# A decoder trunk in three-term fp32r products: the first tile pairs of each feed forward, the weight combinations and the result sums rearranged

## The chip, the cores and the metric

The kernel runs on 1 core of one Trainium2 chip. The metric is device time in microseconds, the median of 3 runs; smaller is better. Engines in the profile: PE (TensorE's matmuls), PEld (its weight loads), DVE (VectorE), ACT (ScalarE), POOL (GpSimd), SP (SyncE, which issues most of the DMAs here).

## What is computed

A trunk of two decoder layers over 512 tokens of 1024 features in float32. Each layer is feed forward, token mixing, feed forward, each with a residual and a layer norm. The first layer mixes by latent attention, the second by sparse attention on keys and values made from the output of the first. The change touches the four feed forwards:

```python
def swiglu(x, w_gu, w_down):
    g, u = jnp.split(x @ w_gu, 2, axis=-1)
    return (jax.nn.silu(g) * u) @ w_down
...
    for layer in range(DEPTH):
        x = layer_norm(DN_ALPHA * x + 0.5 * swiglu(x, ffn_w_gu[layer, 0], ffn_w_down[layer, 0]), ...)
        ... token mixing, w_out, layer_norm ...
        x = layer_norm(DN_ALPHA * x + 0.5 * swiglu(x, ffn_w_gu[layer, 1], ffn_w_down[layer, 1]), ...)
        if layer == N_A_LAYERS - 1:
            shared = nsa_shared_kv(x, ...)
```

with D_FF = 2816, so gate and up are 22 tiles of 128 hidden features each.

## The kernel before, in words

**Products.** Every float32 operand is kept as two fp32r parts, hi (a rounded copy, by ScalarE's cast, L198) and lo (the rest, by VectorE's subtraction, L199); `split` (L194) makes both. A product is three matmuls: hi by hi, hi by lo, lo by hi. The input of a feed forward lies feature-major in `F.xhi` and `F.xlo` (1024 features in 8 blocks of 128, by 512 tokens), and, unsplit, as four raw blocks `F.raw[k, c]` (feature half k, token half c).

**A feed forward** (`ffn`, L456) works through 22 tile pairs (a gate tile and an up tile of 128 hidden features each) in five groups. After each group its down projection adds to the residual (`token_major`, `by_units`, L420 to 453). `GROUPS` (L33) says for each pair of each feed forward which of two ways makes it:

- "s", a plain pair (`single`, L476): two weight units of 128x1024, each `feature_major` (L354): 24 matmuls of 256 columns for each token half, so 96 in all.
- "d", a combined pair (`seven`, L484): a fast multiplication of the 2x2 block matrices (feature halves by token halves), with seven block products of 12 matmuls (`quarter`, L370), 84 in all. Its left operands are g0 to g3: the gate block, the up block and four combinations of their halves (`combined`, L132; four operations of 512 columns on VectorE, in place in the raw weight tiles). Its right operands are `F.xhi`/`F.xlo` quarters and the token forms `F.t[1]` to `F.t[4]`, combinations of the raw blocks (`token_forms`, L385; four subtractions of 1024 columns and four splits). Seven sums of 256 columns on VectorE and one copy on ScalarE put the results together (L494 to 512); then `evac` (L470): Silu on ScalarE, a product on VectorE and a split.

**The front of a feed forward.** The norm that makes the input runs one tile of 128 tokens after the other (`norm_tile`, L318), with transposes on TensorE (L338), so the second token half comes later than the first. In the first, second and fourth feed forward (`halves`, L518 to 534) three plain pairs open: six weight units, first all six on tokens 0 to 255, then all six on tokens 256 to 511. The token forms come behind that, between the next products. The third feed forward reads an `x` that has been there since before the stage ahead of it (`shared_kv`, the keys and values of the second layer); it opens with two plain pairs, and its token forms are started in `shared_kv` (L935).

**Weights.** `unit` (L176) hands out the weight units in the order of `_unit_order` (L53) and prepares up to `look` more ahead (`ahead`, L184; `prep`, L153): a load of 512 KB on SP's queue into one of 4 raw tiles (`wraw`), a cast and a lo subtraction into one of 7 slots. The token forms' subtractions use raw tiles too.

**The start.** The program loads the transposed input in eight pieces (L1262) with one weight unit ahead of it and three between its halves (L1264). The hook `load_x` (L1272) of the first feed forward loads the token-major `x` (four loads pinned to program order) and then the norm's gain and bias, behind the six units of the front.

**What sets the order.** Engines run lists that the compiler orders by readiness with the program's order as priority; tiles of a pool are handed out in program order. PSUM has eight banks, used in turn (`fbank`).

Of the kernel before, what the change touches and what calls it, by code (L numbers as in the profile page):

```python
# [52 lines left out]
def _unit_order():  # L53
# [3 lines left out]
    def ffn(l, f, s):  # L57
        for m0, items in _groups(l, f):
            m = m0
            for it in items:  # L60
# [4 lines left out]
                m += 1  # L65
            for i in range(m0, m):
                order.append(("dn", (l, f, i), 1024, s))
# [36 lines left out]
def tile_trunk(ctx: ExitStack, tc, a: dict, out):  # L104
# [27 lines left out]
    def combined(name, idx):  # L132
# [129 lines left out]
    def open_f(scope):  # L262
# [11 lines left out]
        for i in (1, 2, 3, 0, 4):  # L274
# [181 lines left out]
    def ffn(l, f, i, halves, spill=None, final=False, mid=None, hook=None):  # L456
# [3 lines left out]
        groups = _groups(l, f)  # L460
        for gi, (m0, items) in enumerate(groups):
# [8 lines left out]
            def evac(j, pg, pu, sg=None):  # L470
                sg = sg or hp.tile([P, T], F32, tag="sg", name="sg", bufs=3)
                nc.scalar.activation(sg, pg, AF.Silu)
                nc.vector.scalar_tensor_tensor(sg, sg, 0.5, pu, op0=ALU.mult, op1=ALU.mult)
                split(hhi[:, j, :], hlo[:, j, :], sg)

            def single(j):  # L476
                pp = []
                for g in range(2):
                    w = unit("gu", (l, f, m0 + j, g), 4)
                    pp.append(fbank())  # L480
                    feature_major(w, pp[g], 0, T)
                evac(j, *pp)

            def seven(j):  # L484
# [50 lines left out]
            for it in items:  # L535
                if gi == 0:
                    next(forms, None)
# [934 lines left out]
```

## Time and profile before

| | |
|---|---|
| median of 3 runs | 1878.33 us |
| the runs | 1875.61, 1878.33, 1878.87 us |
| the profiled execution | 1874.17 us, its span 1872.2 us |
| PE, PEld busy | 99%, 88% of the span |
| DVE, ACT, POOL busy | 78%, 46%, 9% |
| mean granted TensorE clock | 0.997 of full speed |

The profile is of one execution. Times in it are us from the span's start. "Busy" counts the time an engine has an instruction in work; matmuls are pipelined, so that the start of one to the start of the next is what one costs, and the printed duration is longer. In a timeline row, `x8` means eight such instructions in a row, and the bracket at the end is the engine's idle time before it and what released it.

### The profile page before, as it was taken

Reading aid. Unit: us, or ns where it says so; the run is one execution under the profiler, and the core shown is the slowest. Engines: PE = TensorE matmul, PEld = TensorE weight load, DVE = VectorE, ACT = ScalarE, POOL = GpSimd, SP = SyncE. Lnnn points to the kernel's source line nnn. Section 1 sums busy time; section 2 is a strip of 40 time slices with the busy share of each in tenths; the row PEclk is TensorE's granted clock in tenths of the full one; section 3 lists DMA queues with packets and bytes.
Section 4 is the critical chain, followed back from the end, with each engine's and each line's share of the span. In section 5 each row is a group of like instructions: output and inputs, shape, how many; then the busy total and the mean of one; then the engine's idle time right before and its main releaser. Section 6 shows DMA issues by size and latency. Waiting matters only on the chain.

```text
span 1872.2 us, 31918 instructions
## 1 busy us (share of the span) xinstructions
PE 1844.3 (99%) x12776; PEld 1650.9 (88%) x12776; DVE 1466.2 (78%) x2362; ACT 869.8 (46%) x1435; POOL 164.2 (9%) x185
## 2 busy tenths in 40 slices
PE   9999999999999999999999999999999999999998
PEld 8899899986679899899999998998956689999997
DVE  8788789757658789788797987987577478888887
ACT  5344345456545345334653433444466345434432
POOL 0000000125500000000100000001255200000000
PEclk9999999999999999999999999999999999999999
DMA  6333335521134234234433323334321224323322
GB/s 245 112 109 126 101 113 158 174 89 35 57 113 136 79 102 136 80 103 145 129 117 113 124 81 112 113 123 154 107 46 28 88 83 146 102 91 113 113 81 78
DMA packets 59700, 203.85 MB, mean 109 GB/s; under 512 B 6944, under 2 KB 7216, under 8 KB 59552
## 3 DMA queue, kind: packets, MB, share of 16 engines
q1 hardware_dynamic: 57136, 194.70, 31.7%
q0 software_dynamic: 2416, 7.11, 1.2%
q8 instruction: 101, 1.65, 0.4%
q14 instruction: 47, 0.39, 0.1%
HBM read 188.16 MB, written 7.34 MB: 104 GB/s over the span
## 4 chain that ended last, share of the span: by engine, by line
PE 92%; DVE 3%; ACT 2%; POOL 1%; issue 1%; DMA 0%; SPq 0%; POOLq 0%; DVEq 0%; ACTq 0%
PE bank L375 13%; PE bank L379 13%; PE bank L376 13%; PE bank L411 5%; PE bank L414 5%; PE bank L412 5%; PE bank L410 5%; PE bank L413 4%; PE bank L415 4%; PE bank L367 3%; PE bank L364 3%; PE bank L362 3%; PE o L645 3%; PE tb L617 3%; PE s L1153 1%; PE bank L352 1%
## 5 line engine op out<-in xcount | busy, mean ns | idle before, releaser
L198 ACT CAST whi<-wraw 128x1024 fp32r<-128x1024 f32 (+3 forms) x479 | 463.2, 976 | 539.2 <-PE bank L415 244.3
L199 DVE TENSOR_TENSOR wlo<-wraw,whi 128x1024 fp32r<-128x1024 f32 (+3 forms) x479 | 536.3, 1126 | 126.6 <-ACT whi L198 125.1
L375 PE MATMUL bank<-t,whi 128*128 128x256 f32 x1232 | 298.4, 278 | 0.0
L376 PE MATMUL bank<-t,whi 128*128 128x256 f32 x1232 | 297.9, 278 | 0.0
L376 PEld LDWEIGHTS bank<-t,whi 128*128 128x128 f32 x1232 | 231.8, 188 | 0.0
L375 PEld LDWEIGHTS bank<-t,whi 128*128 128x128 f32 x1232 | 231.8, 188 | 0.0
L376 PE MATMUL bank<-xlo,whi 128*128 128x256 f32 x924 | 221.9, 277 | 0.0
L375 PE MATMUL bank<-xhi,whi 128*128 128x256 f32 x924 | 221.8, 277 | 0.0
L379 PE MATMUL bank<-t,wlo 128*128 128x256 f32 x1232 | 191.8, 278 | 0.0
L375 PEld LDWEIGHTS bank<-xhi,whi 128*128 128x128 f32 x924 | 173.6, 188 | 0.6
L376 PEld LDWEIGHTS bank<-xlo,whi 128*128 128x128 f32 x924 | 173.6, 188 | 0.6
L379 PEld LDWEIGHTS bank<-t,wlo 128*128 128x128 f32 x1232 | 164.2, 189 | 0.0
L314 DVE SCALAR_TENSOR_TENSOR x<-x,bank 128x512 f32<-128x512 f32 x176 | 112.6, 683 | 57.1 <-PE bank L414 54.3
L379 PE MATMUL bank<-xhi,wlo 128*128 128x256 f32 x924 | 142.9, 277 | 0.0
L411 PE MATMUL bank<-whi,hhi 128*128 128x512 f32 x336 | 131.0, 390 | 0.0
L413 PE MATMUL bank<-wlo,hhi 128*128 128x512 f32 x336 | 130.9, 390 | 0.0
L410 PE MATMUL bank<-whi,hhi 128*128 128x512 f32 x336 | 130.8, 390 | 0.0
L414 PE MATMUL bank<-whi,hlo 128*128 128x512 f32 x336 | 130.8, 389 | 0.0
L412 PE MATMUL bank<-wlo,hhi 128*128 128x512 f32 x336 | 130.8, 389 | 0.0
L362 PE MATMUL bank<-xhi,whi 128*128 128x256 f32 x544 | 130.1, 280 | 0.7 <-ACT xhi L198 0.7
L364 PE MATMUL bank<-xlo,whi 128*128 128x256 f32 x544 | 130.2, 280 | 0.5 <-DVE xlo L199 0.5
L415 PE MATMUL bank<-whi,hlo 128*128 128x512 f32 x336 | 130.7, 389 | 0.0
(330 smaller groups left out, 3548.8 us busy)
## 6 DMA issues: line engine op xcount, KB each, us to landing
wraw<-in_gu SPq DMA_DIRECT2D x175, 512.0 KB, 3.3
wraw<-in_dn SPq DMA_DIRECT2D x88, 512.0 KB, 3.7
wraw<-in_wo SPq DMA_DIRECT2D x16, 512.0 KB, 3.3
wraw<-in_wm SPq DMA_DIRECT2D x8, 512.0 KB, 4.1
x_dram<-x SPq DMA_DIRECT2D x8, 512.0 KB, 3.0
x<-x_dram SPq DMA_DIRECT2D x8, 512.0 KB, 4.4
wraw<-in_w SPq DMA_DIRECT2D x8, 512.0 KB, 4.1
wraw<-in_wq SPq DMA_DIRECT2D x6, 512.0 KB, 3.3
```

The lines of the kernel that those rows point to most:

```text
L198: nc.scalar.copy(hi, src)
L199: eng.tensor_tensor(lo, src, hi.bitcast(F32), op=ALU.subtract)
L364: nc.tensor.matmul(ps[:, c0:c1], lhsT=hi[:, k * P:(k + 1) * P], rhs=F.xlo[:, k, c0:c1], start=False, stop=False)
L375: nc.tensor.matmul(ps, lhsT=hi[:, ks], rhs=xh[:, k], start=k == 0, stop=False)
L376: nc.tensor.matmul(ps, lhsT=hi[:, ks], rhs=xl[:, k], start=False, stop=False)
L379: nc.tensor.matmul(ps, lhsT=lo[:, ks], rhs=xh[:, k], start=False, stop=k == 3)
L410: nc.tensor.matmul(p0, lhsT=ahi, rhs=hi[:, 0:512], start=first, stop=False)
L411: nc.tensor.matmul(p1, lhsT=ahi, rhs=hi[:, 512:1024], start=first, stop=False)
L412: nc.tensor.matmul(p0, lhsT=ahi, rhs=lo[:, 0:512], start=False, stop=False)
L413: nc.tensor.matmul(p1, lhsT=ahi, rhs=lo[:, 512:1024], start=False, stop=False)
L414: nc.tensor.matmul(p0, lhsT=alo, rhs=hi[:, 0:512], start=False, stop=last)
L415: nc.tensor.matmul(p1, lhsT=alo, rhs=hi[:, 512:1024], start=False, stop=last)
```

## The change

- Every feed forward has the same groups, and its first group is one plain pair and four combined ones. Seven plain pairs in all become combined.
- `front` opens each feed forward, the third too: two weight units; the hook; both units on tokens 0 to 255; then `early(1)`, the two quarter products of the next pair that need only g0 and tokens 0 to 255; then the four token forms; then both units on tokens 256 to 511, the plain pair's `evac`, and the rest of the next pair (`seven(1, ...)`). The token forms are no longer spread between products, and those of the third feed forward are no longer started in `shared_kv`.
- The weight combinations add where they subtracted; the signs move to the token forms (two of them by the operation with a scalar, `neg`) and to the factor of `evac`.
- The seven sums of 256 columns become three over 512 columns and one over 256, with the products placed in banks to match (`p15`, `p26`, `p4`, `p37`), and ScalarE's copy stands behind the products with t1, t4 and t2. The two tiles of sums become one of twice the size.
- At the start two units, not three, are prepared between the halves of the transposed input.
- The forms' places in `open_f` are listed in another order.

```diff
@@ -30,14 +30,13 @@
 DMA_RING = 4096
 NRAW, NRING, NEXTRA = 4, 3, 4
 EXTRA = (0, 2, 4, 6)
-GROUPS = (("sssdd", "dddd", "ddddd", "dddd", "dddd"), ("sssdd", "dddd", "ddddd", "dddd", "dddd"),
-          ("ssddd", "dddd", "ddddd", "dddd", "dddd"), ("sssdd", "dddd", "ddddd", "dddd", "dddd"))
-
-
-def _groups(l, f):
+GROUPS = ("sdddd", "dddd", "ddddd", "dddd", "dddd")
+
+
+def _groups():
 
     m, out = 0, []
-    for items in GROUPS[2 * l + f]:
+    for items in GROUPS:
         out.append((m, items))
         m += len(items)
     assert m == NFF
...
@@ -141,13 +138,13 @@
         if name == "g1":
             W.u = load(a["gu"][l, f, m, 1])
             W.s = wraw.tile([P, 1024], F32, name="wraw")
-            op(W.s[:, up], W.g[:, lo], W.u[:, lo], op=ALU.subtract)
+            op(W.s[:, up], W.g[:, lo], W.u[:, lo], op=ALU.add)
             op(W.u[:, lo], W.u[:, lo], W.u[:, up], op=ALU.add)
             return W.u
         if name == "g2":
-            op(W.s[:, lo], W.u[:, lo], W.g[:, lo], op=ALU.subtract)
+            op(W.s[:, lo], W.u[:, lo], W.g[:, lo], op=ALU.add)
             return W.s
-        op(W.g[:, up], W.g[:, up], W.s[:, lo], op=ALU.subtract)
+        op(W.g[:, up], W.g[:, up], W.s[:, lo], op=ALU.add)
         return W.g[:, up]
 
     def prep():
...
@@ -271,7 +268,7 @@
         W.count = 0
         F.fst = ExitStack()
         F.fm = F.fst.enter_context(tc.tile_pool(name=f"fm{scope}", bufs=1, reuse_waits="tile"))
-        for i in (1, 2, 3, 0, 4):
+        for i in (2, 3, 4, 0, 1):
             for e in "hl":
                 if i:
                     F.fm.tile([P, 4, 256], F32, tag=f"t{i}{e}", name="place")
...
@@ -384,9 +381,12 @@
 
     def token_forms():
 
-        def less(x, y):
+        def less(x, y, neg=False):
             u = wraw.tile([P, 1024], F32, name="wraw").rearrange("p (k q) -> p k q", k=4)
-            nc.vector.tensor_tensor(u, x, y, op=ALU.subtract)
+            if neg:
+                nc.vector.scalar_tensor_tensor(u, x, -1.0, y, op0=ALU.mult, op1=ALU.subtract)
+            else:
+                nc.vector.tensor_tensor(u, x, y, op=ALU.subtract)
             return u
 
         def form(i, u):
...
@@ -394,16 +394,12 @@
             split(*F.t[i], u)
 
         b, F.t = F.raw, {}
-        u = less(b[0, 1], b[0, 0])
+        u = less(b[0, 0], b[0, 1])
         form(1, u)
-        yield
-        u = less(b[1, 1], u)
+        u = less(u, b[1, 1], True)
         form(2, u)
-        yield
-        u = less(u, b[1, 0])
-        form(4, u)
-        u = less(b[1, 1], b[0, 1])
-        form(3, u)
+        form(4, less(u, b[1, 0], True))
+        form(3, less(b[1, 1], b[0, 1]))
 
     def prod(ps, w, a, first, last):
         (hi, lo), (ahi, alo), (p0, p1) = w, a, ps
...
@@ -467,82 +463,77 @@
                 F.bk += 1
                 return bank(F.bk - 1)
 
...
+            def hidden():
+                return hp.tile([P, 2, T], F32, tag="sg", name="sg", bufs=2)
+            def evac(j, sg, pg, pu, sign):
                 nc.scalar.activation(sg, pg, AF.Silu)
...
+                nc.vector.scalar_tensor_tensor(sg, sg, 0.5 * sign, pu, op0=ALU.mult, op1=ALU.mult)
                 split(hhi[:, j, :], hlo[:, j, :], sg)
 
...
+            c0, c1 = slice(0, 256), slice(256, 512)
+            def early(j):
                 w = unit("g0", (l, f, m0 + j), 4)
...
+                p15, p26 = fbank(), fbank()
+                quarter(p15[:, c0], w, 0, *quarters(0, 0))
+                quarter(p26[:, c0], w, 512, *quarters(1, 0))
+                return p15, p26
+            def seven(j, p15, p26):
+                both = hidden()
+                gs, us = both[:, 0], both[:, 1]
+                h = both.rearrange("p a (b q) -> p (a b) q", b=2)
+                def sums(o, x, y):
+                    nc.vector.tensor_tensor(o, x, y, op=ALU.add)
+                def twice(x):
+                    return x[:, None, :].to_broadcast([P, 2, 256])
+                def banked(p):
+                    return p.rearrange("p (b q) -> p b q", b=2)
                 w = unit("g1", (l, f, m0 + j), 4)
...
+                p4, p37 = fbank(), fbank()
+                quarter(p15[:, c1], w, 0, *F.t[1])
+                quarter(p4[:, c0], w, 512, *F.t[4])
                 w = unit("g2", (l, f, m0 + j), 4)
...
+                quarter(p26[:, c1], w, 0, *F.t[2])
+                nc.scalar.copy(h[:, 2], p15[:, c0])
+                sums(h[:, 0:4:3], twice(h[:, 2]), banked(p26))
+                quarter(p37[:, c1], w, 512, *F.t[3])
                 w = unit("g3", (l, f, m0 + j), 4)
...
+                quarter(p37[:, c0], w, 0, *quarters(1, 1))
+                sums(h[:, 1:3], twice(h[:, 3]), banked(p37))
+                sums(h[:, 1:4:2], h[:, 1:3], twice(p15[:, c1]))
+                sums(h[:, 2], h[:, 2], p4[:, c0])
+                evac(j, gs, gs, us, -1)
+            def front():
+                ws = [unit("gu", (l, f, m0, g), 0) for g in range(2)]
+                ps = [fbank() for _ in range(2)]
                 if hook is not None:
                     hook()
                     load_gb(l, i, nc.sync)
                 for c in range(2):
                     for w, p in zip(ws, ps):
                         feature_major(w, p, c * 256, c * 256 + 256)
...
+                    if c == 0:
+                        pp = early(1)
+                        token_forms()
+                evac(0, hidden()[:, 0], *ps, 1)
+                seven(1, *pp)
+            if gi == 0:
+                front()
+            for j in range(2 if gi == 0 else 0, n):
+                seven(j, *early(j))
 
             last = gi == len(groups) - 1
             if gi == 2 and mid is not None:
...
@@ -932,7 +923,6 @@
         nc.gpsimd.dma_start(b1, a["cmp_b1"].to_broadcast([64, 2, 256]))
         ws = [unit("wkf", (i,), 4) for i in range(4)]
         ps = [bank(i) for i in range(4)]
-        F.forms = token_forms()
         for c in range(2):
             for i in range(4):
                 feature_major(ws[i], ps[i], c * 256, c * 256 + 256)
...
@@ -1263,7 +1253,7 @@
                 k = slice(e * 4 + i.start, e * 4 + i.stop)
                 split(F.xhi[:, k, q], F.xlo[:, k, q], xr[:, i])
         if c == 0:
-            for i in range(3):
+            for i in range(2):
                 prep()
     sst.close()
     nc.vector.tensor_copy(cbf[:, 0:256], cst[:, 0:256])
...
@@ -1292,11 +1282,11 @@
     open_f(1)
     out_proj(0)
     mst.close()
-    ffn(0, 1, 2, True)
+    ffn(0, 1, 2)
     zst, zp = right_pool("zp")
     shared_kv(zp)
     zst.close()
-    ffn(1, 0, 0, False, spill=x_dram[1])
+    ffn(1, 0, 0, spill=x_dram[1])
     F.fst.close()
     F.mix = {}
     mst, F.mp = right_pool("mix1")
...
@@ -1315,7 +1305,7 @@
     open_f(2)
     out_proj(1)
     mst.close()
-    ffn(1, 1, 2, True, final=True)
+    ffn(1, 1, 2, final=True)
     F.fst.close()
     close_f()
     PS.left_st.close()
```

The lines that the long hunk takes out (`single`, `seven` and the old front) are in the listing above.

## Rows read from the trace of the kernel before

**Rows 1.** The page's first part: busy us (share of span), instructions by engine

```profile
PE 1844.3 (99%) x12776; PEld 1650.9 (88%) x12776; DVE 1466.2 (78%) x2362; ACT 869.8 (46%) x1435; POOL 164.2 (9%) x185
```

**Rows 2.** The page's chain that ended last, by engine

```profile
PE 92%; DVE 3%; ACT 2%; POOL 1%; issue 1%; DMA 0%; SPq 0%; POOLq 0%; DVEq 0%; ACTq 0%
```

**Rows 3.** Timeline of PE, first and second front: start us, us, engine, line, operation

```profile
18.68 1.07 PE L367 MATMUL bank<-xhi,wlo 128*128 128x256 f32 x8
...
21.40 1.07 PE L367 MATMUL bank<-xhi,wlo 128*128 128x256 f32 x8
22.30 0.28 PE L362 MATMUL bank<-xhi,whi 128*128 128x256 f32 x1
...
594.71 0.28 PE L375 MATMUL bank<-xhi,whi 128*128 128x256 f32 x1
...
604.31 0.28 PE L375 MATMUL bank<-xhi,whi 128*128 128x256 f32 x1
```

**Rows 4.** Timeline of PE, second and fourth front, around the last token tiles

```profile
560.71 0.36 PE L362 MATMUL bank<-xhi,whi 128*128 128x256 f32 x1
...
570.34 1.06 PE L338 MATMUL bank<-cst,x 128*128 128x128 f32 x8
571.15 0.36 PE L364 MATMUL bank<-xlo,whi 128*128 128x256 f32 x1
...
1526.07 0.28 PE L362 MATMUL bank<-xhi,whi 128*128 128x256 f32 x1
...
1528.59 0.36 PE L364 MATMUL bank<-xlo,whi 128*128 128x256 f32 x1
...
1537.04 1.09 PE L338 MATMUL bank<-cst,x 128*128 128x128 f32 x8
```

**Rows 5.** Timeline of DVE, second front: the last token tile and the forms

```profile
571.62 1.29 DVE L199 TENSOR_TENSOR xlo<-bank,xhi 128x512 fp32r<-128x512 f32 x2 [1.37 <-ACT xhi L198]
572.97 1.23 DVE L389 TENSOR_TENSOR wraw<-b 128x1024 f32<-128x1024 f32 x1
...
575.44 1.22 DVE L199 TENSOR_TENSOR t<-wraw,t 128x1024 fp32r<-128x1024 f32 x1
...
577.71 1.22 DVE L199 TENSOR_TENSOR t<-wraw,t 128x1024 fp32r<-128x1024 f32 x1
...
579.98 2.48 DVE L199 TENSOR_TENSOR t<-wraw,t 128x1024 fp32r<-128x1024 f32 x2
```

**Rows 6.** Timeline of SP's queue and of ACT at the start

```profile
0.73 0.87 SPq L129 DMA_DIRECT2D wraw<-in_gu  x2
...
15.06 0.33 SPq L297 DMA_DIRECT2D b<-in_ln_b  x1
...
9.86 1.05 ACT L198 CAST whi<-wraw 128x1024 fp32r<-128x1024 f32 x1 [0.58 <-DMA wraw<-in_gu]
```

**Rows 7.** DMA issues: tensor, queue, count, KB each, us from issue to landing

```profile
b<-in_ln_b SPq DMA_DIRECT2D x1, 512.0 KB, 11.2
```

**Rows 8.** Timeline of DVE, behind the second front: sums, combination, hidden product

```profile
616.08 0.41 DVE L506 TENSOR_TENSOR us<-us,bank 128x256 f32<-128x256 f32 x1
616.41 0.42 DVE L512 TENSOR_TENSOR gs<-gs,bank 128x256 f32<-128x256 f32 x1
...
618.54 0.69 DVE L150 TENSOR_TENSOR wraw<-wraw 128x512 f32<-128x512 f32 x1
619.14 0.69 DVE L473 SCALAR_TENSOR_TENSOR gs<-gs,us 128x512 f32<-128x512 f32 x1
```

**Rows 9.** Timeline of PE, where the third feed forward opens

```profile
949.46 0.31 PE L994 MATMUL bank<-cst,hb 64*128 64x64 f32 x2 [2.42 <-DVE hb L991]
...
954.16 1.73 PE L367 MATMUL bank<-xhi,wlo 128*128 128x256 f32 x8
```

**Rows 10.** Two stretches: us, busy us (xcount) by engine, granted clock, DMA share, GB/s

```profile
561.00:614.00 53.00, 53.00 (x465) 52.99 (x464) 46.94 (x61) 29.92 (x41) 1.71 (x3) 1.00 0.39 130
952.00:966.00 14.00, 14.00 (x111) 13.72 (x109) 12.60 (x22) 6.21 (x14) 0.00 (x0) 0.88 0.12 37
```

More of the change, by code (lines that the diff above doesn't have):

```diff
@@ L57, in ffn @@
     def ffn(l, f, s):
-        for m0, items in _groups(l, f):
-            m = m0
-            for it in items:
+        for m0, items in _groups():
+            for m, it in enumerate(items, m0):
                 if it == "d":
@@ L64, in ffn @@
                     order.extend(("gu", (l, f, m, g), 1024, s) for g in range(2))
-                m += 1
-            for i in range(m0, m):
-                order.append(("dn", (l, f, i), 1024, s))
+            for m in range(m0, m0 + len(items)):
+                order.append(("dn", (l, f, m), 1024, s))
     ffn(0, 0, 0)
@@ L453, in by_units, with ffn @@
                         on_tile(t, ps[t])
-    def ffn(l, f, i, halves, spill=None, final=False, mid=None, hook=None):
+    def ffn(l, f, i, spill=None, final=False, mid=None, hook=None):
         hst, hp = right_pool(f"h{l}{f}")
@@ L459, in ffn @@
             load_gb(l, i)
-        groups = _groups(l, f)
+        groups = _groups()
         for gi, (m0, items) in enumerate(groups):
@@ L474, in evac @@
                 split(hhi[:, j, :], hlo[:, j, :], sg)
[L476 to L484, printed above, removed]
-                c0, c1 = slice(0, 256), slice(256, 512)
-                gs = hp.tile([P, T], F32, tag="sg", name="gs", bufs=3)
-                us = hp.tile([P, T], F32, tag="sg", name="us", bufs=3)
-                op = nc.vector.tensor_tensor
-                w = unit("g0", (l, f, m0 + j), 4)
-                p12 = fbank()
-                quarter(p12[:, c0], w, 0, *quarters(0, 0))
-                quarter(p12[:, c1], w, 512, *quarters(1, 0))
-                nc.scalar.copy(us[:, c0], p12[:, c0])
-                op(gs[:, c0], us[:, c0], p12[:, c1], op=ALU.add)
+            c0, c1 = slice(0, 256), slice(256, 512)
@@ L496, in seven @@
                 w = unit("g1", (l, f, m0 + j), 4)
-                p45 = fbank()
-                quarter(p45[:, c0], w, 512, *F.t[4])
-                quarter(p45[:, c1], w, 0, *F.t[1])
+                p4, p37 = fbank(), fbank()
+                quarter(p15[:, c1], w, 0, *F.t[1])
+                quarter(p4[:, c0], w, 512, *F.t[4])
                 w = unit("g2", (l, f, m0 + j), 4)
-                p67 = fbank()
-                quarter(p67[:, c0], w, 0, *F.t[2])
-                quarter(p67[:, c1], w, 512, *F.t[3])
@@ L504, in seven @@
-                op(us[:, c0], us[:, c0], p67[:, c0], op=ALU.add)
-                op(gs[:, c1], us[:, c0], p45[:, c1], op=ALU.add)
-                op(us[:, c0], us[:, c0], p67[:, c1], op=ALU.add)
-                op(us[:, c1], us[:, c0], p45[:, c1], op=ALU.add)
-                op(us[:, c0], us[:, c0], p45[:, c0], op=ALU.subtract)
-                w = unit("g3", (l, f, m0 + j), 4)
-                p3 = fbank()
-                quarter(p3[:, c0], w, 0, *quarters(1, 1))
-                op(gs[:, c1], gs[:, c1], p3[:, c0], op=ALU.add)
@@ L513, in seven @@
-                evac(j, gs, us, gs)
-            j = 0
-            if gi == 0:
-                forms = token_forms() if halves else F.forms
-            if gi == 0 and halves:
-                ws, ps = [], []
-                for j in range(3):
-                    for g in range(2):
-                        ws.append(unit("gu", (l, f, m0 + j, g), 0))
-                        ps.append(fbank())
+                quarter(p26[:, c1], w, 0, *F.t[2])
+                nc.scalar.copy(h[:, 2], p15[:, c0])
@@ L529, in ffn @@
                         feature_major(w, p, c * 256, c * 256 + 256)
-                for j in range(3):
-                    next(forms, None)
-                    evac(j, ps[2 * j], ps[2 * j + 1])
-                j = 3
-                items = items[3:]
-            for it in items:
-                if gi == 0:
-                    next(forms, None)
-                if it == "d":
-                    if gi == 0:
-                        for _ in forms:
-                            pass
-                    seven(j)
-                else:
-                    single(j)
-                j += 1
+                    if c == 0:
[7 more added lines that the diff above has]
+                seven(j, *early(j))
             last = gi == len(groups) - 1
@@ L1274, in load_x @@
             tc.keep_in_program_order(nc.sync.dma_start(F.x[t], a["x"][t]))
-    ffn(0, 0, 0, True, spill=x_dram[0], mid=memory_load, hook=load_x)
+    ffn(0, 0, 0, spill=x_dram[0], mid=memory_load, hook=load_x)
     F.fst.close()
```

3 lines of the change are left out of this document (removed).

## The prediction

> **What bounds the kernel now.** I read the page's first part, then the chain of waits, then TensorE's groups by line, then the stretches around the four places where a feed forward opens. In the first part the reader sees TensorE busy for 99% of the span, its weight loads for 88% and VectorE for 78% [rows 1]. A busy TensorE says little by itself, since the ends of its matmuls are modelled, so the chain is next: 92% of it are matmuls, with VectorE at 3% [rows 2]. TensorE is the bound, and a matmul that is left out is worth its start-to-start time wherever nothing else ends last. That time I read from the starts: eight matmuls of one line follow each other every 2.72 us, with 16 others between, so 24 matmuls of 256 columns take 2.72 us, 0.113 us each [rows 3]. A combined tile pair ("seven", 84 matmuls) takes 604.31 - 594.71 = 9.60 us [rows 3]; a plain one has 96, 4 x 2.72 = 10.88 us. Between the parts TensorE hardly pauses, busy as it is for 99% [rows 1].
>
> **What goes.** Seven plain pairs become combined ones (two in each of three feed forwards, one in the third). Each gives 10.88 - 9.60 = 1.28 us, so 7 x 1.28 = **9.0 us less of matmuls**: 2.56 us in each feed forward but the third, 1.28 us there. The number of weight loads from DRAM stays, two per pair of either sort.
>
> **What that work covered.** In the first, second and fourth feed forward the plain pairs' first halves gave TensorE work that needs only tokens 0 to 255, while the other half was still on its way. Six units of 2.72 us are 16.3 us. The change leaves two units and the quarter products of the next pair's g0, three times 2.72 = 8.16 us. I go through the four fronts.
>
> Second feed forward. The first product starts at 560.71, so the three blocks end at 568.87. The next work on TensorE is the transposes of token tile 3, which start at 570.34, when VectorE has finished that tile [rows 4]: 1.47 us of pause. Before, those 1.47 us were products. Then the second half needs the low parts of x, whose splits run from 571.62 to 572.91 [rows 5]. TensorE is free at 571.15 and can work at its pace from about 572.3, another 1.1 us. Together 2.6 us.
>
> Fourth. Nine matmuls run from 1526.07 on, before tile 2's transposes; the other 63 run from 1528.59 and take 7.14 us, to 1535.73. Tile 3's transposes come at 1537.04 [rows 4], 1.3 us later, and the same split adds 1.1: 2.4 us.
>
> First. Here the combined weights are late. TensorE has done two units, the early block and the second halves at 22.30 (the same 2.72 us steps as now) [rows 3]. The next product needs the second weight block u, whose load stands on SP's queue behind the four loads of x and the two of the norm's gain and bias. Now the last of these is issued at 15.06 and lands 11.2 us later, at 26.3, with 8 MiB moved since the first issue at 0.73 [rows 6, 7]: 3.2 us per MiB. Up to u there will be 7 MiB, so it lands at about 23.1. Two additions of 0.69 us [rows 8] and a cast of 1.05 us [rows 6] follow, and the product can start at 25.6: a wait of 3.3 us. Were u issued ahead of x, the wait would be none; the loads of x are pinned to program order, so I take the 3.3.
>
> Third. x was ready long before; no wait for tokens. The token forms leave the stage ahead of it, where TensorE waits 2.42 us for the end of a chain on VectorE [rows 9]. One of their subtractions, 1.23 us [rows 5], may stand in that chain now, and a weight split can take its place; I count 0, between -1.2 and +1.
>
> **The token forms.** Now they are made during the third to sixth unit's products. In the second feed forward they run from 572.97 to 582.46, 9.5 us [rows 5], and cannot start sooner: they need the same last tile. After the change the second halves end at 572.3 + 5.44 = 577.7. The first form is ready at 576.66, the second (t2) at 578.93, t4 at about 581.2, t3 at 582.46 [rows 5]. If TensorE takes the products as written (t1, t4, t2, t3, then the one without a form), it waits 581.2 - 579.1 = 2.1 us. If the compiler's order puts t2 and the free one ahead of t4, it waits for nothing. Between 0 and 2.1 I take 0.8, nearer to 0, because the order is by readiness elsewhere too: the matmuls written behind tile 3's transposes run ahead of them now [rows 4]. The same 0.8 in the third and fourth; in the first the wait for u covers it.
>
> **Additions and sums.** Subtract becomes add on the same sizes, and two of the four token subtractions take the scalar form, which lasts as long as the plain one (0.69 us each for 512 columns [rows 8]): nothing. Seven sums of 256 columns become three of 512 and one of 256. One lasts 0.42 or 0.69 us, but the next starts 0.33 or 0.60 us after it (616.41 after 616.08, 619.14 after 618.54 [rows 8]): 7 x 0.33 = 2.31 against 3 x 0.60 + 0.33 = 2.13 us per pair, 0.2 us of VectorE. In the steady groups TensorE covers VectorE, so it is worth 0; it counts in rival 3.
>
> **VectorE behind the front.** Each further combined pair costs it four additions and splits of 3.5 blocks, 4 x 0.60 + 3 x 1.14 + 0.60 = 6.4 us (1.14 for 1024 columns: two such operations pass between 575.44 and 577.71 [rows 5]), 2.1 us of sums and 1.2 us for the hidden product: 9.7 us, against 9.6 on TensorE. Now it is busy for 46.9 of 53 us in the second front [rows 10] and already prepares later units there. I take 0 for its lag, with 0.5 us per pair (2 per front) as the other end.
>
> **Sum.** First -2.56 + 3.3 = +0.7; second -2.56 + 2.6 + 0.8 = +0.8; third -1.28 + 0.8 = -0.5; fourth -2.56 + 2.4 + 0.8 = +0.6. Together **+1.6 us**. The profiled execution took 1874.17 us, 1872.2 of it span; it would be 1875.8. That execution is 4.2 us under the median of the runs, 1878.33, and I forecast for the median: 1879.9, rounded to **1880.0 us**. A measurement of this kernel can tell some 0.2%, 3.8 us, so that is no change.
>
> **Rivals.**
> 1. Faster: the covers hold. u goes out ahead of x, forms are taken in the order of readiness, and only the two waits for tile 3 stay: -9.0 + 2.6 + 2.4 = -4.0, 1874.3 us; without those too, 1869.3. For it: TensorE's order already follows readiness [rows 4], and VectorE has idle time ahead of tile 3 in which the pair's weights can be combined. Against it: tile 3 itself does not come sooner.
> [...]
> 3. Slower: VectorE ends last behind the front. A lag of 0.5 us per pair, over the 4 pairs of a first group, in 4 fronts, is +8 on top of +1.6: 1887.9; half of it where VectorE can put off preparation for the down products: 1883.9. It decides from the point where VectorE's 9.7 us per pair are no longer met by spare time. For it 9.7 against 9.6 us; against it the spare time [rows 10]. [...]
> 4. Slower: the order stays as written. Then it is 2.1 us instead of 0.8 in three fronts, +3.9: 1883.9. For it that the products are written with t4 second; against it the order by readiness in [rows 4]. [...]
>
> **How the numbers follow.** The forecast (within 0.2%) 0.44; rival 1 0.28; rival 2 0.12, rival 3 0.10 and rival 4 0.06, which gives 0.28 for slower by over 0.2%. The range holds most of the rivals' cases: from between rival 1's two times, 1872, to 1887, past rivals 2 and 4 and most of rival 3. The forecast's own range is 1874.6 to 1882.1.
>
> **What would show it.** Right: 84 matmuls of 256 columns fewer; in the second and fourth front a pause of 1 to 1.5 us before the transposes of tile 3; in the first a pause on u's addition after some 22 us; the steady groups unchanged. Rival 1: no pause, each down projection's start 2 us earlier after its front. [...] Rival 3: TensorE waiting on casts or splits of weights in the third and fourth pair. The prediction is wrong if the waits sum to less than 5 or more than 13 us.

## The result, and the profile after

The changed kernel takes **1888.32 us** (median; 1888.08 to 1889.78) against 1878.6 us (1875.61 to 1881.42) for the kernel before: ratio 1.0054, 95% interval 1.0036 to 1.0071. It is slower by some 10 us, where 1880.0 and no change were forecast; the range ended at 1887.

The page's first part and its chain answer to [rows 1, 2]:

```profile
PE 1846.3 (98%) x12692; PEld 1646.6 (87%) x12692; DVE 1489.5 (79%) x2201; ACT 888.3 (47%) x1456; POOL 166.1 (9%) x185
...
PE 87%; DVE 6%; issue 2%; ACT 2%; POOL 1%; DMA 1%; POOLq 0%; SPq 0%; DVEq 0%; ACTq 0%
```

84 matmuls are gone as forecast, but the matmuls' share of the chain fell from 92 to 87%, and VectorE's doubled to 6%. To find where, I cut both traces at matmuls that both have: the start of the first down projection of each feed forward (rows like the one below), the last product ahead of its last down projection, and the first product of each output projection. Differences of these starts, in us:

```profile
72.48 0.39 PE L406 MATMUL bank<-whi,hhi 128*128 128x512 f32 x1
```

| stretch | before | after | change | forecast |
|---|---|---|---|---|
| start to first down projection (first front) | 60.55 | 72.48 | +11.9 | +0.7 |
| groups 1 to 5, first feed forward | 261.53 | 261.54 | 0 | 0 |
| first attention | 200.13 | 201.17 | +1.0 | 0 |
| second front | 91.70 | 92.34 | +0.6 | +0.8 |
| its groups | 261.54 | 262.15 | +0.6 | 0 |
| third front (with the stage ahead of it) | 129.21 | 126.45 | -2.8 | -0.5 |
| second attention | 221.80 | 224.56 | +2.8 | 0 |
| fourth front | 92.54 | 92.86 | +0.3 | +0.6 |

The groups of the third and fourth feed forward are 261.54 in both traces, and the end is 0.1 shorter. With it the rows add up, but for rounding, to the 14.4 us between the two spans (1872.2 and 1886.6). The medians are 9.7 apart, since the trace of before is of an execution 4 us under its median. The 0.6 us in the groups of the second feed forward are not explained: no wait of TensorE is listed there. **The first front alone is worse by more than the whole change.**

The timeline of PE and, below it, of DVE shows the first front after the change.

```profile
23.23 1.07 PE L364 MATMUL bank<-xhi,wlo 128*128 128x256 f32 x8
31.36 0.58 PE L372 MATMUL bank<-xhi,whi 128*128 128x256 f32 x1 [7.05 <-ACT whi L195]
...
41.40 0.39 PE L372 MATMUL bank<-t,whi 128*128 128x256 f32 x1 [0.68 <-ACT t L195]
```

```profile
24.42 0.69 DVE L471 SCALAR_TENSOR_TENSOR sg<-sg,bank 128x512 f32<-128x512 f32 x1 [8.17 <-PE bank L364]
25.79 0.69 DVE L196 TENSOR_TENSOR hlo<-sg,hhi 128x512 fp32r<-128x512 f32 x1 [0.68 <-ACT hhi L195]
26.40 0.69 DVE L141 TENSOR_TENSOR wraw<-wraw 128x512 f32<-128x512 f32 x1
...
33.19 1.22 DVE L389 TENSOR_TENSOR wraw<-b 128x1024 f32<-128x1024 f32 x1
...
41.86 1.22 DVE L196 TENSOR_TENSOR t<-wraw,t 128x1024 fp32r<-128x1024 f32 x1
```

TensorE has nothing to do for 7.05 us. VectorE stands still for 8.17 us before 24.42, until TensorE's second halves have ended (the releaser in the bracket), then does the plain pair's product and split first, u's combinations from 26.40 on, and the token forms only from 33.19 to 43, although their inputs were there by 14.9, when the last cast of the transposed input ends. The windows add the clock (columns as in [rows 10]); the first row is of the kernel before, the others are of the change:

```profile
10.00:15.00 5.00, 5.00 (x45) 4.95 (x44) 3.95 (x4) 4.55 (x6) 0.00 (x0) 1.00 1.04 410
...
10.00:15.00 5.00, 5.00 (x31) 5.00 (x32) 4.01 (x6) 4.44 (x7) 0.00 (x0) 0.66 1.03 404
25.00:31.30 6.30, 0.00 (x0) 0.00 (x0) 5.51 (x8) 4.07 (x5) 0.00 (x0) 0.67 0.00 0
31.30:38.00 6.70, 6.64 (x32) 6.46 (x33) 6.67 (x8) 2.12 (x4) 0.00 (x0) 0.55 0.00 0
```

In the change the granted clock is twice at a low level, the second time from within the pause on: 0.50 from 10.2 to 13.3 and from 28 to 37 us. By the means in the windows that is 0.34 x 5 / 0.5 = 3.4 us of it in the first stretch and 0.45 x 6.7 / 0.5 = 6.0 us in the third. Half of it is lost (matmul starts 0.21 us apart from 31.74 to 32.38, 0.11 from 22.78 to 23.23, at 1.00): an estimate of 1.7 and 3.0 us. Account of the first front: 24 matmuls less -2.7, the wait +7.05, clock +4.7, two waits for forms with their restarts +1.2 (starts 0.42 and 0.84 late), which is +10.3 of +11.9; where the other 1.6 us lie was not traced.

In the second front the pauses are those of the forecast: 1.04 us before tile 3's transposes and two shorter ones behind them; no wait for a form.

```profile
583.91 1.09 PE L335 MATMUL bank<-cst,x 128*128 128x128 f32 x8 [1.04 <-DVE x L330]
585.24 0.50 PE L359 MATMUL bank<-xhi,whi 128*128 128x256 f32 x2 [0.24 <-ACT xhi L195]
585.96 0.39 PE L361 MATMUL bank<-xlo,whi 128*128 128x256 f32 x1 [0.23 <-DVE xlo L196]
```

### The profile page after: what moved, and what is told of

Its sections match the earlier page's. It is cut to its first block, busy times and chain, and to the rows that moved or that the text cites. A ratio compares the mean times of both kernels' runs of the same rounds, so it can differ in the third digit from the quotient of the medians.

```text
span 1886.6 us, 31578 instructions
## 1 busy us (share of the span) xinstructions
PE 1846.3 (98%) x12692; PEld 1646.6 (87%) x12692; DVE 1489.5 (79%) x2201; ACT 888.3 (47%) x1456; POOL 166.1 (9%) x185
## 4 chain that ended last, share of the span: by engine, by line
PE 87%; DVE 6%; issue 2%; ACT 2%; POOL 1%; DMA 1%; POOLq 0%; SPq 0%; DVEq 0%; ACTq 0%
PE bank L372 14%; PE bank L373 14%; PE bank L376 14%; PE bank L410 4%; PE bank L406 4%; PE bank L407 4%; PE bank L408 4%; PE bank L409 4%; PE bank L411 4%; PE o L636 3%; PE tb L608 3%; PE bank L361 2%; PE bank L364 2%; PE bank L359 1%; PE bank L348 1%
## 5 line engine op out<-in xcount | busy, mean ns | idle before, releaser
L372 PE MATMUL bank<-t,whi 128*128 128x256 f32 x1344 | 327.0, 279 | 1.4 <-ACT t L195 0.9
L373 PE MATMUL bank<-t,whi 128*128 128x256 f32 x1344 | 326.1, 278 | 0.4 <-DVE t L196 0.3
L372 PEld LDWEIGHTS bank<-t,whi 128*128 128x128 f32 x1344 | 253.1, 188 | 2.4 <-ACT t L195 1.3
L373 PEld LDWEIGHTS bank<-t,whi 128*128 128x128 f32 x1344 | 253.1, 188 | 1.4 <-DVE t L196 1.2
L372 PE MATMUL bank<-xhi,whi 128*128 128x256 f32 x1008 | 244.3, 278 | 7.4 <-ACT whi L195 7.4
L373 PE MATMUL bank<-xlo,whi 128*128 128x256 f32 x1008 | 243.9, 278 | 0.0
L492 DVE TENSOR_TENSOR sg<-sg,bank 128x512 f32<-128x512 f32 x336 | 206.2, 614 | 4.5 <-PE bank L376 2.7
L376 PE MATMUL bank<-t,wlo 128*128 128x256 f32 x1344 | 209.5, 278 | 0.0
L373 PEld LDWEIGHTS bank<-xlo,whi 128*128 128x128 f32 x1008 | 190.6, 189 | 0.6
L324 POOL TENSOR_TENSOR st<-st,cst 128x1 f32<-128x1 f32 x24 | 20.2, 843 | 1492.6 <-DVE st L323 1492.5
L376 PEld LDWEIGHTS bank<-xhi,wlo 128*128 128x128 f32 x1008 | 134.7, 189 | 0.2 <-DVE wlo L196 0.2
L408 PE MATMUL bank<-wlo,hhi 128*128 128x512 f32 x336 | 130.8, 389 | 0.0
```

What stands on the lines that cost most here:

```text
L372: nc.tensor.matmul(ps, lhsT=hi[:, ks], rhs=xh[:, k], start=k == 0, stop=False)
L373: nc.tensor.matmul(ps, lhsT=hi[:, ks], rhs=xl[:, k], start=False, stop=False)
L376: nc.tensor.matmul(ps, lhsT=lo[:, ks], rhs=xh[:, k], start=False, stop=k == 3)
L408: nc.tensor.matmul(p0, lhsT=ahi, rhs=lo[:, 0:512], start=False, stop=False)
L492: nc.vector.tensor_tensor(o, x, y, op=ALU.add)
```

## The experiments

Each is a change to the kernel after, unless said otherwise. "First front" is the start of the first down projection.

**u ahead of x (e1).**

```diff
-                if hook is not None:
-                    hook()
-                    load_gb(l, i, nc.sync)
...
                         pp = early(1)
+                        if hook is not None:
+                            hook()
+                            load_gb(l, i, nc.sync)
                         token_forms()
```

> The changed kernel, but in the first feed forward the loads of x and of the norm's gain and bias are put behind the preparation of the next pair's weights, so that u's load stands ahead of them on SP's queue. Theory A (u is late, and VectorE's list behind it): u lands after 4 MiB instead of 7, near 14 us instead of 24; the wait of 7.2 us at 31.4 goes, VectorE's idle 8.2 us before 24.4 are used, and the first down projection starts at 59.5 to 62 instead of 72.5: 11 to 13 us less, 1875 to 1878 in all. Theory B (VectorE cannot keep the pace of four combined pairs, whenever u comes): only part of the wait goes, the first down projection starts at 66 or later and the time stays above 1882. Theory C (what is lost is the clock at the start, 6.6 to 13.4 us at the low level): under 3 us less.

Measured: 1879.6 us (ratio to before 1.0013, 1.0004 to 1.0023), 8.7 us less than the change; first front 63.73. The timeline of DVE, and TensorE's waits from 10 to 60 us:

```profile
16.04 0.68 DVE L141 TENSOR_TENSOR wraw<-wraw 128x512 f32<-128x512 f32 x1
...
21.69 1.22 DVE L389 TENSOR_TENSOR wraw<-b 128x1024 f32<-128x1024 f32 x1
...
30.75 1.22 DVE L196 TENSOR_TENSOR t<-wraw,t 128x1024 fp32r<-128x1024 f32 x1
```

```profile
PE bank L372 <- ACT t L195: 1.1, 2, 0.7
PE bank L372 <- ACT whi L195: 0.5, 1, 0.5
```

u's combinations start 10 us sooner, the 7 us wait is gone: theory A. But it fell 1.7 us short of its 62. Two causes offer themselves. VectorE is busy for 14.97 and 15.00 us of the two stretches 30 to 45 and 45 to 60, so B may have a part. And the start ran longer at the low clock: 0.68 from 6 to 10 us and 0.57 from 10 to 15, against 1.00 and 0.66 in the change's trace, which by the same reckoning loses 3.4 us instead of 1.7 (theory C's low stretch in the change, put at 6.6 to 13.4 us, is 10.1 to 13.4 in that trace). The runs below come back to both.

**The forms' differences in tiles of their own (e2)**, only in the first feed forward; u behind x.

```diff
-            u = wraw.tile([P, 1024], F32, name="wraw").rearrange("p (k q) -> p k q", k=4)
+            u = own.pop(0)
...
+                            t0 = hp.tile([P, 4, 256], F32, tag="tmp", name="tmp")
+                            t1 = hidden().rearrange("p a (b q) -> p (a b) q", b=2)
+                            own = [t0, t1, t0, t1]
```

> The changed kernel, but in the first feed forward the differences for the token forms go to tiles of their own instead of the four raw weight tiles; u stays behind x. Theory A2 (two causes: u is late, and the forms wait for the raw tile that g0 holds until u's combinations are done): the forms are made between 16 and 25 us, the 7.2 us wait for u's combinations stays within 1 us, the three waits for forms of 1.5 us and the slow pace behind them go, and the first down projection starts near 69 instead of 72.5: 3 to 4 us less, 1884 to 1885. If u alone is the cause: no difference beyond 1 us.

Measured: 1883.89 us, 4.4 less than the change; first front 66.77. The first form's difference starts at 15.59 instead of 33.19:

```profile
15.59 1.22 DVE L392 TENSOR_TENSOR tmp<-b 128x1024 f32<-128x1024 f32 x1
...
25.91 0.68 DVE L141 TENSOR_TENSOR wraw<-wraw 128x512 f32<-128x512 f32 x1
```

So the raw tile did hold the forms back for 17 us. TensorE's one wait is now 4.8 us, where I expected the 7.2 to stay: a product with g1 can run as soon as g1 is cast, where in the change it lacked its form too. There are two causes, not u alone.

**The plain pair's `evac` written behind the rest of the next pair (e3).**

```diff
-                evac(0, hidden()[:, 0], *ps, 1)
                 seven(1, *pp)
+                evac(0, hidden()[:, 0], *ps, 1)
```

> The changed kernel, but in every front the plain pair's Silu, product and split are written behind the rest of the next pair, so that VectorE's list has u's combinations first. If u's landing (13.6 + 10.3 = 23.9 us) is what the wait ends on once the list allows it: combinations start at 24 instead of 26.4, the first down projection 2.5 us sooner, 1885.8. If the list order costs nothing because the casts behind it decide: within 0.5 us of the changed kernel. In the other fronts both expect less than 0.5 us.

Measured: 1887.36 us, 1.0 less than the change, between the two expectations; first front 70.38, 2.1 less, of which the groups behind it give back 1.5 (263.05 us).

```profile
23.95 0.69 DVE L141 TENSOR_TENSOR wraw<-wraw 128x512 f32<-128x512 f32 x1 [7.94 <-DMA wraw<-in_gu]
```

This dates u's landing: 23.9, 0.8 later than forecast. In the change the combination stood 2.45 us in VectorE's list behind a product that waited for TensorE. Not all of that is the price of the order: in the change's trace TensorE's second halves came late, with the clock at 0.66 from 10 to 15 us, where this trace has 1.00. By its loads u is there at 23.9 in the change's trace too (issued from 13.56 on, 10.3 us to land), and its addition starts at 26.40, behind that product at 24.42 and its split at 25.79.

**Both of the first two edits (e4).**

> Both edits of the first two runs. Theory A2: no wait is left in the first front but those of the start, 312 matmuls of 0.113 us behind 24.1 us: the first down projection at 59.5, 1 to 2 us less than with u ahead of x alone, 1874 to 1877 in all. Theory A (u alone): the same as with u ahead of x alone, within 0.7 us. Theory B: as with u ahead of x alone, above 1882.

Measured: 1880.39 us, within the interval of the first edit alone; first front 62.90, 0.8 less, which is less than its start gained by the clock (0.92 and 0.72 in the two stretches, where the first edit alone had 0.68 and 0.57: some 1.7 us). A wait of 1.4 us for a form stays. With u early the raw tile hardly matters.

**Two plain pairs in the first feed forward (e5)**, u ahead of x (`ns` is the number of "s" in the first group). At the start three units, not two, are again prepared between the halves of the transposed input, here and in all runs below that start with two plain pairs.

```diff
-                ws = [unit("gu", (l, f, m0, g), 0) for g in range(2)]
+                ws = [unit("gu", (l, f, m0 + j, g), 0) for j in range(ns) for g in range(2)]
...
-                        pp = early(1)
+                        pp = early(ns)
```

> As the run with u ahead of x, and the first feed forward alone opens with two plain pairs, then the early products (444 matmuls to its first down projection, 12 more). Theory B2 (with u early, VectorE's work is what still holds the first front, at 63.7 instead of the 58 us or so that TensorE needs): a plain pair less to combine frees some 6 us of VectorE, the waits for forms go, and the first down projection starts at 58.5 to 60.5: 3 to 5 us less than with u ahead of x, 1875 to 1877. Theory D (the forms' own waits and the slow start decide, not VectorE's load): 12 matmuls more, so 1.4 us later, near 65 and 1881.

Measured: 1876.08 us (0.9991, 0.9982 to 1.0); first front 62.02, no wait left behind 10 us. 12 matmuls more and 1.7 us sooner: 3.1 us of waits and slowly paced products went, 1.6 of them waits in the list above, while the clock at the start is as low as with u ahead alone. So VectorE's load was what was left (B2), though 62.0 misses the expected 60.5. The reason is the start:

```profile
6.00:10.00 4.00, 2.22 (x6) 1.34 (x6) 2.54 (x5) 1.98 (x4) 0.00 (x0) 0.67 1.01 366
10.00:15.00 5.00, 5.00 (x27) 5.00 (x28) 3.96 (x5) 3.96 (x5) 0.00 (x0) 0.58 1.04 411
```

27 matmuls in 5 us, where the kernel before had 45: 0.33 x 4 / 0.5 = 2.6 and 0.42 x 5 / 0.5 = 4.2 us at the low level, half of it lost, an estimate of 3.4 us.

**A longer warm-up (e9)** on top: 16 instead of 12 matmuls on zeros.

> As the run with two plain pairs in the first feed forward and u ahead of x, with 16 instead of 12 matmuls on zeros ahead of the first products. In that run the clock stood at the low level from 7.3 to 14.2 us, behind the thin products that wait for the first splits of x; the kernel before shows no such stretch. Theory: with the zeros' matmuls up to 8 us instead of 6.3 the granted clock stays at the high level, 0.5 to 1 us of products start later and 3.4 us are won: the first down projection at 59 to 60 instead of 62.0, 1873 to 1874.5. Rival: the thin products behind it drop the clock all the same, only later: 62 to 63, no gain.

Measured: first front 58.93, with the clock at 1.00 in both stretches, as the theory says for one execution; but 1875.98 us, 0.1 less than without. The median shows nothing of the 3.1 us, and this trace lost 1.2 us in the second attention. A trace below speaks against the warm-up as the cause: e10, whose code and order of instructions in this front are those of e5, with 12 matmuls on zeros, has the clock at 1.00 in both stretches too, and a first front of 60.06. So the start's low clock comes in some executions of one and the same code; what decides on it stays open.

**Two plain pairs, u behind x (e8)** (the loads as in the change).

> Two plain pairs in the first feed forward, with x's loads where the change has them, ahead of u. Theory A: TensorE has work until 33 us or so, u lands after 8 MiB at 26 to 27, so that the 7.2 us wait is gone by cover alone; but the forms still wait for g0's raw tile, and the first down projection starts 1 to 4 us later than with u ahead, 60 to 64. If only u's place on the queue matters: still a wait of more than 3 us before u's product, 66 or later.

Measured: 1884.24 us, first front 68.67: later than theory A's 60 to 64 and above the 66 of the other, but without the wait for u that the other asks for.

```profile
28.21 0.69 DVE L472 SCALAR_TENSOR_TENSOR sg<-sg,bank 128x512 f32<-128x512 f32 x1 [10.66 <-PE bank L365]
```

```profile
PE bank L373 <- ACT t L196: 3.5, 4, 1.4
```

VectorE idles 10.66 us, with the plain pair's product at the head of its list, and the waits are for forms. Cover for u alone does not help. The run does not part u from g0, though: four units are loaded ahead of x, so g0's load stands behind x as well.

**Two plain pairs in three feed forwards (e6)**, one in the third.

> Two plain pairs and the early products in the first, second and fourth feed forward, one plain pair in the third, u ahead of x. In the second and fourth front five blocks of 2.72 us cover the last token tile, so that its pauses of some 2 us go for 1.36 us of matmuls: each 0.5 to 1.3 us less than in the changed kernel. Expected by my account of the fronts: 1873 to 1876, faster than both kernels. If the pauses only move (the second half's splits or the forms end last all the same): the second and fourth front 1.4 us longer than in the changed kernel, 1877 to 1880.

Measured: 1876.89 us. It misses the expected 1873 to 1876. The second front is 90.60 (1.7 less than in the change) and the fourth 92.72 (0.1 less, where 0.5 to 1.3 were expected): the second's pauses are covered, the fourth's gain is not there. And the third, whose code is the same, is 132.85, with a new wait:

```profile
PE bank L360 <- DVE skc L197: 4.9, 1, 4.9
```

**The kernel before, again (e7).**

> The kernel before, unchanged, for a second trace. If the stages between the feed forwards that were 1.0 and 2.8 us longer after the change (the first attention, the second) differ by that much from one execution of the kernel before to another, they will here be some 1 to 3 us longer than in its first trace, while the fronts stay within 0.5 us. If the change made them longer, they stay within 0.5 us of the first trace.

Measured: attention stages 200.48 and 221.53, first front 60.48, second 91.68, fourth 92.63: within 0.4. Only the third front differs, 131.12. So the longer attention stages belong to the change.

**The weight slots moved, in the attention stages and in the stage ahead of the third feed forward (e10, e11).** The first edit stands on two plain pairs in the first feed forward (e5), the second, with `("wkf", (0,)): 2` alone, on two in three (e6).

```diff
+SHIFT = {("wm", (0, 0)): 5, ("wgq", (0,)): 5}
...
         name, idx, n, scope = order[W.done]
+        W.count += SHIFT.get((name, idx), 0)
```

> As the run with two plain pairs in the first feed forward and u ahead of x, and the count that deals out the seven weight slots is moved by 5 where the two attention stages begin, so that their weights take the slots they took in the kernel before. Theory P (the stages between the feed forwards got 0.8 and 2.0 us longer because each feed forward now uses another number of weight units, so that another slot is next): first attention at 200.1 to 200.5 instead of 201.0, second at 221.5 to 221.8 instead of 223.8, 2 to 3 us less in all, 1873.5 or so. Rival (the raw tiles, the banks or the order are the cause): both stages as they were, within 0.4 us.

Measured: 1874.04 us, 2.0 less; first attention 200.72, second 222.13. The second is below all eleven traces of the change and its variants without this edit (223.15 to 225.03). But the edit does not do there what I expected of it. The slot is the count's remainder by seven. Counted along the units' order, the second attention begins at remainder 1 in the kernel before and 0 in the change; with this edit it begins at 5, so it leaves the change's slots without taking the old ones. The traces say that 0 is the bad one. In the ten that begin at 0 TensorE waits 0.9 us for a tile `mix`, in the six that begin at 1, 3 or 5 it waits 0.2; the first row is of the change, the second of this run:

```profile
PE o L694 <- DVE mix L196: 0.9, 1, 0.9
PE o L699 <- DVE mix L199: 0.2, 1, 0.2
```

The ten take 223.50 to 225.03 us, the six 221.20 to 223.15. So the slots are shown to be a cause in the second attention. In the first the edit does restore the old remainder (0), and the stage moves by 0.2 us of the 0.8: slots are not its main cause, and what is stays open.

> As the run with two plain pairs in three feed forwards, with the same count moved by 2 where the stage ahead of the third feed forward begins, so that its weights take the slots that they take in the changed kernel. Theory P: the 6.4 us that this stage lost there (132.85 instead of 126.46 us from the second feed forward's last products to the third's first down projection, with a wait of 5.1 us and a stretch at the low clock) are a matter of slots: back to 126.4 to 127.4, 1870.5 to 1871.5 in all. Rival: within 1 us of 132.85, 1877.

Measured: third front 133.13, 1880.12 us. Slots are not its cause. The second attention begins at remainder 0 here, at 5 without this edit, and is 1.5 us longer (224.64 against 223.15), with the wait for `mix` at 0.9 again.

**The PSUM bank in which the third feed forward begins (e12, e14).** The new wait names `skc`, a tile of the stage ahead, which ends in banks 4 and 5. `fbank` counts on from one feed forward to the next: 82 calls before (bank 2), 86 in the change (bank 6), 84 with two plain pairs (bank 4).

```diff
+        if (l, f) == (1, 0):
+            F.bk += 4
```

In the kernel before:

> The kernel before, with the count that deals out the eight PSUM banks moved by 4 where the third feed forward opens, so that its products begin in bank 6, as in the changed kernel, and no longer in bank 2, which the stage ahead of it holds until its chain on VectorE has ended. Theory K (what the change won in the third front beyond its 1.36 us of matmuls comes from the bank): the 2.4 to 3 us wait ahead of the transposes of hb is filled with products, no stretch at the low clock, second feed forward's last products to third's first down projection 126 to 127.5 us instead of 129.2 to 131.1, 1873.5 to 1875.5 in all. Rival (it comes from the forms' subtraction having left VectorE's chain, as bounded in the prediction): 129 or more.

Measured: **1872.05 us** (0.9967, 0.9958 to 0.9977), third front 124.86, both better than expected. TensorE's waits from 940 to 980, which answer to the 2.42 us of [rows 9], and the timeline of PE around the transposes of hb:

```profile
PE bank L996 <- DVE hb L993: 0.3, 1, 0.3
```

```profile
951.11 0.75 PE L367 MATMUL bank<-xhi,wlo 128*128 128x256 f32 x5
951.79 0.34 PE L996 MATMUL bank<-cst,hb 64*128 64x64 f32 x2
952.06 0.62 PE L367 MATMUL bank<-xhi,wlo 128*128 128x256 f32 x3
```

Products of the feed forward stand ahead of the transposes and behind them, and the clock from 952 to 966 is 1.00, where [rows 10] has 0.88.

In the changed kernel, whose products then begin in bank 2:

> The changed kernel, with the third feed forward's products beginning in bank 2 as in the kernel before. Theory K: the wait for hb comes back, 128.5 to 131 us instead of 126.45, 1890 to 1892 in all. Rival: 126.4 to 127.4, 1888.

Measured: 1891.22 us, third front 129.46, 3.0 more:

```profile
PE bank L986 <- DVE hb L983: 1.9, 1, 1.9
```

Theory K holds both ways. In banks 2 and 3 the stage ahead still holds the tiles for hb's transposes, so the feed forward's products do not run ahead of them (a wait of 2.42 us in [rows 9], 1.9 here); in bank 6 they fill that wait.

**Two plain pairs in three feed forwards, the bank (`F.bk += 2`) and the attention's slots (e13).**

> Two plain pairs and the early products in the first, second and fourth feed forward, one in the third, u ahead of x, the third feed forward's banks as in the changed kernel (bank 6 instead of 4), and the weight slots of the two attention stages moved by 5. Theory K: the 6.4 us of the third front go (126.4 to 127.5 instead of 132.85), the attention stages win 1 to 2 us as in the run with the slots alone: 1868 to 1871 in all, faster than both kernels. If the bank is not the cause: 1875 to 1878.

Measured: 1871.8 us (0.9968, 0.9957 to 0.998), third front 127.31, attention stages 200.74 and 221.43 (the second from remainder 3), first front 62.26. It is faster than both kernels, 16.5 us under the change, but 0.8 above the upper end of what I expected; the first front with its slow start (7.78 us to the first products, the clock at 0.77 and 0.50 in the two stretches) is 2 us over that of e10, whose start is the same code at 1.00. The kernel before with only its bank moved does as well, within the two intervals.

## Why the prediction was wrong

**The first front** failed: "First -2.56 + 3.3 = +0.7" was +11.9. The 11.2 us are more than the whole miss (8.3 us by the medians). The step that failed is the wait of 3.3 us, which counted u's own chain alone; it was 7.05 us, with the clock and the forms' waits behind it. u's landing was right to 0.8 us (23.9 against 23.1). Three things behind it were not:
- "Two additions of 0.69 us [rows 8] and a cast of 1.05 us [rows 6] follow, and the product can start at 25.6". VectorE's list had the plain pair's product ahead of the additions, and that waits for TensorE's second halves: 2.45 us in the trace (run e3: 2.1 less in its first front, 1.0 in the median).
- "in the first the wait for u covers it", the wait for the forms. It did the reverse. The forms' differences take raw tiles, dealt out in order behind g0, u, their sum and the next g0; the next in turn is g0's, which is held until u's combinations are done. So VectorE idled through u's wait and had 9 us of forms to do after it (e2, with tiles of their own: first front 5.7 us less, 4.4 in the median). With both products of g1 lacking a form, TensorE's first product was the next pair's, whose cast is the last of four.
- The clock is rival 2, with a chance of 0.12. My estimate, from the 0.88 in 952 to 966 us behind the wait of 2.42 us [rows 9, 10], was 1.7 us lost in each of three fronts, 1885.0 in all, and the range was drawn to hold it. No run shows it in three fronts. In the changed kernel a low clock behind a pause came in the first alone, where the pause is 7.05 us in one piece: 3.0 us, plus 1.7 at the start, which no forecast had. The three traces of the kernel before have 1.00 from 10 to 15 us, the three of the change's own start (the change, e3, e14) 0.66, 1.00 and 0.78; so that part differs between executions, and whether the change brings it is not shown. In the second and fourth front of the changed kernel the granted clock stays at 1.00 (575 to 628 and 1538 to 1560 us), with waits of 1.04 and 1.3 us for tile 3.

The alternative was in the text: "Were u issued ahead of x, the wait would be none". Run e1 makes that change, and 1879.6 us is the forecast's number, though the first front, 3.2 us over before, is not its +0.7.

**Matmuls, second and fourth front.** 84 matmuls fewer, as forecast; +0.6 and +0.3 against +0.8 and +0.6. The sums are right, with some luck in the terms. In the second the pause before tile 3 was 1.04 us against 1.47, with two short ones of 0.5 together where 1.1 us was allowed, and no wait for a form came, where the order as written would have cost 2.1 us: rival 4 fell there. TensorE's listed waits grew by 1.9 us in this front (0.5 to 2.3) and by 1.8 in the fourth (1.0 to 2.7), where 3.4 and 3.2 were forecast; the other 1.3 to 1.5 us are not in any listed wait and stay unnamed.

**The third front** came out 2.3 us better than forecast (4.2 by the second trace of before), for a reason that the prediction did not name. It bounded the forms' subtraction in VectorE's chain; what decided was the bank. With the bank as before, the change gives 129.46 against 129.21 and 131.12: within what was forecast. With bank 6 in both, 126.45 against 124.86: by these two traces the change itself costs 1.6 us there.

**The stages between** were forecast at 0 and cost 1.0 and 2.8 us. The change moved their weights to other slots; the runs show that as a cause in the second attention and leave the first open.

**Additions and sums**: worth 0 as forecast. The groups that have nothing but combined pairs take 261.54 us before and after (262.15 in one of the four), with four sums per pair of 614 ns on average, 2.46 us, for seven of 0.42 us, 2.94 us:

```profile
L492 DVE TENSOR_TENSOR sg<-sg,bank 128x512 f32<-128x512 f32 x336 | 206.2, 614 | 4.5 <-PE bank L376 2.7
```

By durations that is 0.48 us a pair; the starts in [rows 8] had promised 0.2. Nothing on TensorE's path shows either.

**Rival 3** (VectorE ends last) was right in kind for the first front once u is early: it is busy throughout from 30 to 60 us in e1, and one combined pair less took 3.1 us of waits and slow products away. In the other fronts no wait of its kind showed.

## What to carry to other kernels

Before counting a wait once, ask which buffers its holder keeps: a late load in a shared rotation of raw tiles stops also the work behind it that needs none of it, here 9 us of token forms. Read the order of VectorE's list, not only the moment when data is there. And when the number of tiles in one stage changes, look at which bank and which slot the next stage begins in: one line that moved the bank gave the old kernel 5.9 us.

## What the runs showed of the hardware

- Two loads of 512 KB, issued from 13.6 us on behind 6.5 MiB on the same queue, took 10.3 us to land (the median of the two); the median of all 175 such loads is 3.3 us before and after.

```profile
wraw<-in_gu SPq DMA_DIRECT2D x2, 512.0 KB, 10.3
```

- TensorE's granted clock at the start differs between executions of one and the same code. Up to the first attention e5 and e10 do not differ; from 6 to 10 us TensorE started 6 matmuls in one and 16 in the other, and from 10 to 15 us the granted clock was 0.58 and 1.00. With four more matmuls on zeros (e9) it was 1.00 as well, after 21. The rows of e10, then those of e9, beside those of e5 above:

```profile
6.00:10.00 4.00, 2.71 (x16) 1.83 (x14) 3.90 (x7) 2.79 (x5) 0.00 (x0) 1.00 1.01 400
10.00:15.00 5.00, 5.00 (x43) 5.00 (x43) 4.17 (x4) 4.57 (x7) 0.00 (x0) 1.00 1.03 408
...
6.00:10.00 4.00, 3.73 (x21) 2.40 (x20) 3.35 (x6) 2.94 (x5) 0.00 (x0) 1.00 1.03 410
10.00:15.00 5.00, 5.00 (x46) 5.00 (x46) 4.32 (x5) 4.51 (x7) 0.00 (x0) 1.00 1.03 405
```
